# A decoder layer on one core: feed-forward units taken in pairs, seven block products in place of eight

## The chip, the core and the metric

The kernel runs on one core of a Trainium2 chip. The engines named here are PE (TensorE, matmuls into PSUM), DVE (VectorE), ACT (ScalarE), POOL (GpSimd) and SP, which only issues transfers between DRAM and SBUF. Each engine takes its instructions in a fixed order and waits, at each, until what the instruction needs is there. The metric is device microseconds of one execution, lower is better; the median of three runs before is 626.39 us (626.0 to 626.81).

## The reference

One layer of a decoder on 256 tokens of width 1024, in float32: two mixers (blockwise attention and a gated recurrence), cross-attention to 256 memory tokens, a SwiGLU feed-forward part with 2816 hidden columns, and a final norm. What the change touches is the feed-forward part:

```
hn = rmsnorm(h, norm_ffn_g[l])
gu = hn @ w_ffn_in[l]
h = h + (jax.nn.silu(gu[..., :FFN_HIDDEN]) * gu[..., FFN_HIDDEN:]) @ w_ffn_out[l]
return rmsnorm(h, final_norm_g)
```

## The kernel before, in words

**Chunks.** All weights are laid out as 97 chunks of 1 MB, a tile of 128 x 2048 each, in the order of use (`ORDER`, from `plan`). Chunks 0 to 63 belong to the stages ahead of the feed-forward part, 33 to it. A chunk is loaded by SP into a `raw` tile (two buffers), and then split into two float32r tiles: `hi`, a rounded copy by ACT (L193), and `lo`, the rest, raw minus hi (L197). Both are made in two halves; of each half of 1024 columns DVE computes 576 of `lo` and POOL 448 (in the first nine chunks DVE computes all). There are three buffers of `hi` and of `lo`. A product of two float32 matrices is then three float32r matmuls, hi by hi, lo by hi and hi by lo (`mm3t`, L236 to L239). `nxt` (L204) hands out the next chunk and first prepares all chunks up to two ahead (`LEAD`).

**The feed-forward part.** The hidden columns are cut into 11 units of 256. A unit's input chunks `("I", o, kh)` hold 512 of the 1024 rows (`kh` is the half) and its 256 gate and 256 up columns. For both halves `kh` and both halves `t` of the tokens (128 each), `ffn_in` adds 4 x 3 matmuls of 128 x 512 into the PSUM tile `psi` of that `t`: 24 matmuls for a chunk. The normed input stands transposed as `h2h` and `h2l` (made from `h2g` in `turn_h2`); its scale by token, `r`, is applied behind the product. `gate` (L1092) makes `fu` = silu(r * gate) * (r * up), by one row of ACT and one of DVE. `turn_hid` transposes the two `fu` of a unit on PE (`hidT`) and splits them into `hid`. The unit's output chunk `("O", o)` is 2 x 1024; `ffn_out` adds its 24 matmuls into four PSUM tiles `acc` that stay for the whole part. The order on PE is: the two input chunks of unit o, with the transposes of unit o - 1 between them, then the output chunk of unit o - 1.

**Order.** PE's order is that of the code. For the other engines a scheduler decides, except in the last few lines of the kernel. PSUM is eight banks: four in the pool `mm`, where `psi` and `hidT` are, and four in `sm`, where `acc` is in this part.

Of the kernel before, what the change touches and what calls it, by code (L numbers as in the profile page):

```python
# [10 lines left out]
F32 = mybir.dt.float32  # L11
# [56 lines left out]

ORDER = plan()


# [46 lines left out]
def build(tc, A, out):  # L118
    nc = tc.nc
    V, SC, G, PE, SY = nc.vector, nc.scalar, nc.gpsimd, nc.tensor, nc.sync  # L120
    with ExitStack() as ctx:
# [43 lines left out]
        ready = {}  # L165
        made, at = [0], [0]

        def prep(tags=None, raw=None):
            i = made[0]
            made[0] += 1  # L170
            first = i < 2
            if raw is None:
                raw = wr.tile([128, 2048], F32, name="raw", tag="raw")
            if tags is None:
# [11 lines left out]
            if sent == 1:  # L186
                SY.dma_start(raw, A["w"][i])
            for c in range(pieces):
                a = slice(c * n, (c + 1) * n)
                if i == 0:  # L190
                    SY.dma_start(raw[:, a], piece(A["w"][i], a))
                    yield
                SC.activation(hi[:, a], raw[:, a], AF.Copy)  # L193
                cut = (c + 1) * n - (0 if i in ALONE else POOL_COLS // pieces)
                for eng, b in ((V, slice(c * n, cut)), (G, slice(cut, (c + 1) * n))):
                    if b.start < b.stop:
                        eng.tensor_tensor(lo[:, b], raw[:, b], hi[:, b].bitcast(F32), op=ALU.subtract)  # L197
            ready[i] = (hi, lo)

        def run(g):  # L200
            for _ in g:
                pass

        def nxt(lead=LEAD):  # L204
            i = at[0]
            at[0] += 1
            while made[0] <= min(i + lead, len(ORDER) - 1):
                run(prep())
            return ready.pop(i)

# [24 lines left out]

        def mm3t(ps, xh, xl, h, l, first, last):  # L236
            PE.matmul(ps, xh, h, start=first, stop=False)  # L237
            PE.matmul(ps, xh, l, start=False, stop=False)  # L238
            PE.matmul(ps, xl, h, start=False, stop=last)  # L239

# [821 lines left out]
        def wo_part(ps, t, c, kh):  # L1062
            t_part(ps, wo[2 * c + kh], (oxh, oxl), t, kh)

        def turn_h2(t, c):
# [8 lines left out]
            G.tensor_tensor(h2l[:, ks, ts], g, h2h[:, ks, ts].bitcast(F32), op=ALU.subtract)  # L1074

        todo = None
# [10 lines left out]

        ring = ("B7", "B14", "B10", "B11", "B12", "B6")
        X2 = (h2h, h2l)
        hid, acc, two, psi, hm = {}, {}, {}, {}, {}  # L1090

        def gate(o, t):  # L1092
            r, ps = two["r"][:, t:t + 1], psi.pop((o, t))
            g = t2("fg", (128, 256))
            SC.activation(g, ps[:, 0:256], AF.Silu, scale=r)  # L1095
            u = t2b("fu", (128, 256))
            V.scalar_tensor_tensor(u, ps[:, 256:512], r, g, op0=ALU.mult, op1=ALU.mult)  # L1097
            hm[o, t] = u

        def turn_hid(o):  # L1100
            bk = mm.tile([128, 2, 256], F32, name="hidT", tag="mm")
            for t in range(2):
                u = hm.pop((o, t))
                for j in range(2):
                    PE.transpose(bk[:, j, t * 128:(t + 1) * 128], u[:, j * 128:(j + 1) * 128], ident)
            hd = big(ring[o % 6], "hid", (128, 2, 2, 256), F32R)
            split(bk, hd[:, 0], hd[:, 1])
            hid[o] = hd

        def ffn_in(o, kh, t, w):  # L1110
            if kh == 0:
                psi[o, t] = mm.tile([128, 512], F32, name="psi", tag="mm")
            t_part(psi[o, t], w, X2, t, kh)

# [9 lines left out]

        def ffn_out(o):
            w = by_k(nxt(), 2)
            for t in range(2):
                for c in range(2):
                    out_part(o, w, t, c)

        for u in ORDER[at[0]:-2]:
            if u[0] == "O":
                ffn_out(u[1])
                continue
            _, o, kh = u
            w = by_k(nxt(), 4)
            for t in range(2):
                ffn_in(o, kh, t, w)
                if (o, kh, t) == (0, 0, 0):
                    turn_h2(1, 1)  # L1140
                    two["r"] = rstd2(ssq2, "h2")
                if kh == 1:
                    gate(o, t)
            if kh == 0 and o:
                turn_hid(o - 1)

# [18 lines left out]
        ssq3 = cp.tile([128, 5], F32, name="ssq3")  # L1165
        hg3 = {i: big(ring[j], "hg3", (128, 512)) for j, i in enumerate(((0, 0), (0, 1), (1, 0)))}
        v3 = cp.tile([128, 3], F32, name="v3")
# [94 lines left out]
```

## Time and profile before

| | |
|---|---|
| median of the runs | 626.39 us |
| span of the profiled execution | 624.0 us |
| outside the span | 2.4 us |
| first feed-forward matmul | 432.0 us |
| mean granted clock of TensorE | 0.997 |
| DMA | 107.5 MB, mean 172 GB/s |

The span is one profiled execution, from its first instruction to its last. In the rows of groups, the columns are: line, engine, operation, out<-in, shapes, count, then busy us and mean ns of one, then the idle time before them and what ended it. A tile's rows give minimum, median and maximum of the duration in ns, then the first and last start. A timeline row begins with start and duration in us. Lines of the kernel before and of the changed kernel differ; L193 before is L257 after, L197 is L261, L279 is L347.

### The profile page before, as it was taken

Reading aid. Unit: us, or ns where it says so; the run is one execution under the profiler, and the core shown is the slowest. Engines: PE = TensorE matmul, PEld = TensorE weight load, DVE = VectorE, ACT = ScalarE, POOL = GpSimd, SP = SyncE. Lnnn points to the kernel's source line nnn. Section 1 sums busy time; section 2 is a strip of 40 time slices with the busy share of each in tenths; the row PEclk is TensorE's granted clock in tenths of the full one; section 3 lists DMA queues with packets and bytes.
Section 4 is the critical chain, followed back from the end, with each engine's and each line's share of the span. In section 5 each row is a group of like instructions: output and inputs, shape, how many; then the busy total and the mean of one; then the engine's idle time right before and its main releaser. Section 6 shows DMA issues by size and latency. Waiting matters only on the chain.

```text
span 624.0 us, 8466 instructions
## 1 busy us (share of the span) xinstructions
PE 615.9 (99%) x3135; PEld 512.5 (82%) x3135; DVE 384.2 (62%) x672; ACT 331.4 (53%) x533; POOL 372.4 (60%) x296
## 2 busy tenths in 40 slices
PE   9999999999999999999999999999999999999995
PEld 7888888888877877778888889888888888888884
DVE  7566678979766875748856456754444444444433
ACT  7775554234376756727457556644543444434432
POOL 3887844556544464355867876656655665566553
PEclk9999999999999999999999999999999999999998
DMA  9755443334443333545455544453344555454511
GB/s 345 296 204 202 155 182 135 135 135 140 185 149 135 136 135 134 204 169 183 156 207 189 183 175 189 140 199 134 132 178 171 195 203 187 166 190 198 203 68 67
DMA packets 16888, 107.50 MB, mean 172 GB/s; under 512 B 2000, under 2 KB 2640, under 8 KB 4560
## 3 DMA queue, kind: packets, MB, share of 16 engines
q1 hardware_dynamic: 16128, 106.14, 46.5%
q10 hardware_dynamic: 720, 0.84, 0.4%
q8 instruction: 24, 0.39, 0.3%
q14 instruction: 16, 0.13, 0.1%
HBM read 105.92 MB, written 1.05 MB: 171 GB/s over the span
## 4 chain that ended last, share of the span: by engine, by line
PE 98%; DVE 0%; POOL 0%; issue 0%; POOLq 0%; DVEq 0%
PE pst L237 14%; PE pst L239 14%; PE pst L238 14%; PE psi L237 6%; PE psi L239 6%; PE psi L238 6%; PE psf L252 5%; PE acc L237 3%; PE acc L239 3%; PE acc L238 3%; PE psf L253 2%; PE lp L616 2%; PE psg L510 1%; PE pso L237 1%; PE pso L239 1%; PE pso L238 1%
## 5 line engine op out<-in xcount | busy, mean ns | idle before, releaser
L197 POOL TENSOR_TENSOR lo<-raw,hi 128x448 fp32r<-128x448 f32 x172 | 272.6, 1602 | 182.1 <-ACT hi L193 169.6
L193 ACT ACTIVATE hi<-raw 128x1024 fp32r<-128x1024 f32 (+1 forms) x194 | 195.7, 1036 | 165.9 <-PE pst L239 58.9
L197 DVE TENSOR_TENSOR lo<-raw,hi 128x576 fp32r<-128x576 f32 (+2 forms) x194 | 198.1, 1027 | 133.6 <-ACT hi L193 131.6
L237 PE MATMUL pst<-hi,Xh 128*128 128x512 f32 x256 | 103.2, 403 | 0.0
L239 PE MATMUL pst<-hi,Xl 128*128 128x512 f32 x256 | 99.9, 390 | 0.0
L238 PE MATMUL pst<-lo,Xh 128*128 128x512 f32 x256 | 99.8, 390 | 0.0
L237 PE MATMUL psi<-hi,h2h 128*128 128x512 f32 x176 | 69.6, 395 | 0.0
L239 PE MATMUL psi<-hi,h2l 128*128 128x512 f32 x176 | 68.7, 390 | 0.0
L238 PE MATMUL psi<-lo,h2h 128*128 128x512 f32 x176 | 68.5, 389 | 0.0
L239 PEld LDWEIGHTS pst<-hi,Xl 128*128 128x128 f32 x256 | 48.0, 188 | 10.4
L237 PEld LDWEIGHTS pst<-hi,Xh 128*128 128x128 f32 x256 | 48.1, 188 | 9.9 <-issue 0.7
L238 PEld LDWEIGHTS pst<-lo,Xh 128*128 128x128 f32 x256 | 48.1, 188 | 9.3
L239 PEld LDWEIGHTS psi<-hi,h2l 128*128 128x128 f32 x176 | 33.0, 188 | 7.1
L238 PEld LDWEIGHTS psi<-lo,h2h 128*128 128x128 f32 x176 | 33.1, 188 | 6.6
L237 PEld LDWEIGHTS psi<-hi,h2h 128*128 128x128 f32 x176 | 33.1, 188 | 6.5
L237 PE MATMUL acc<-hi,hid 128*128 128x512 f32 x86 | 33.6, 390 | 0.0
L239 PE MATMUL acc<-hi,hid 128*128 128x512 f32 x86 | 33.5, 389 | 0.0
L238 PE MATMUL acc<-lo,hid 128*128 128x512 f32 x86 | 33.5, 389 | 0.0
L1097 DVE SCALAR_TENSOR_TENSOR fu<-psi,r_h,fg 128x256 f32<-128x256 f32 x22 | 10.6, 484 | 26.0 <-ACT fg L1095 26.0
L1095 ACT ACTIVATE fg<-psi,r_h 128x256 f32<-128x256 f32 x22 | 10.4, 475 | 29.9 <-PE psi L239 29.9
L252 PE MATMUL psf<-H,hi 128*128 128x512 f32 x64 | 22.8, 400 | 0.0
L252 PE MATMUL psf<-M,hi 128*128 128x512 f32 x64 | 22.5, 396 | 0.0
(344 smaller groups left out, 1120.9 us busy)
## 6 DMA issues: line engine op xcount, KB each, us to landing
raw<-w SPq DMA_DIRECT2D x94, 1024.0 KB, 4.8
raw<-w SPq DMA_DIRECT2D x4, 512.0 KB, 6.1
raw<-w SPq DMA_DIRECT2D x4, 256.0 KB, 4.1
H<-xtok SPq DMA_DIRECT2D x1, 1024.0 KB, 9.2
mraw<-mT SPq DMA_DIRECT2D x1, 1024.0 KB, 5.0
xraw<-xT SPq DMA_DIRECT2D x1, 512.0 KB, 6.1
gfin<-gfin SPq DMA_DIRECT2D x1, 512.0 KB, 3.7
out<-H SPq DMA_DIRECT2D x2, 256.0 KB, 2.0
```

The lines of the kernel that those rows point to most:

```text
L193: SC.activation(hi[:, a], raw[:, a], AF.Copy)
L197: eng.tensor_tensor(lo[:, b], raw[:, b], hi[:, b].bitcast(F32), op=ALU.subtract)
L237: PE.matmul(ps, xh, h, start=first, stop=False)
L238: PE.matmul(ps, xh, l, start=False, stop=False)
L239: PE.matmul(ps, xl, h, start=False, stop=last)
L252: PE.matmul(ps, w[0][:, k, a], X2[:, :, k], start=k == 0, stop=False)
L253: PE.matmul(ps[:, 0], w[1][:, k, a], X2[:, 0, k], start=False, stop=k == 7)
L510: PE.matmul(pss[c][t], z[:, k, t * 128:(t + 1) * 128], ws[c][0][:, k], start=z is Xh and k == 0, stop=False)
L616: PE.matmul(ps[:, j], KS[:, a0 + j], QQ[:, a0 + j, 0:n], start=True, stop=True)
L1095: SC.activation(g, ps[:, 0:256], AF.Silu, scale=r)
L1097: V.scalar_tensor_tensor(u, ps[:, 256:512], r, g, op0=ALU.mult, op1=ALU.mult)
```

## The change

**Products.** Unit 0 stays as it was. Units 1 to 10 become five pairs (a, b) (`PAIRS`). For a pair, tokens (two halves), rows (two halves) and units (two) make a product of 2 x 2 blocks by 2 x 2 blocks, which took eight block products of 12 matmuls (half an input chunk's work each). It is now done with seven, in Winograd's form of Strassen's scheme. Four of the seven left sides are sums of the blocks of `h2g`; `token_sums` makes and splits them once (`ts`, `Sh`). The right sides are four chunks as they are and three sums of chunks.

**Sums of chunks.** For each pair two sums of two chunks are made in DRAM (`summed`), by POOL's transfers: a copy of one chunk and then a transfer that adds another. These 20 transfers are issued one at each odd chunk from 9 to 47 (`block_sums`, called in `nxt`). Product 5 loads the first sum (and, beside it, the chunk of product 3) into a double tile `raws`. Product 6's weights are `raws[0]` plus `raws[1]`, added by DVE over 2048 columns (L218); product 4's are that plus one more chunk, which a transfer of POOL adds into SBUF (L221). Product 7 loads the second sum.

**Banks and gates.** Products 1, 6, 7 and 4 add up in one PSUM tile, `b1`; ACT copies it on the way, behind products 1, 6 and 7 (`fc`). Product 2 is in `b2`; products 5 and 3 add up in `b3`. DVE combines copies and banks into the four blocks of gate and up columns. The order on PE is 1, 2, 5, 6, an output chunk, 7, an output chunk, 4, 3, with the transposes of the pair before behind 1 and 2; in the first pair there is one output chunk, behind 7. `gate` now makes two rows of ACT (silu, and a scaled copy of up) and multiplies on POOL.

**Buffers.** In this part every second `raw` goes to two more buffers (`more`, at the places of two tiles that held the weights of the stage just ahead), so there are four. `hid` has four places in place of six. DVE computes all columns of `lo` from chunk 64 on, and POOL none.

```diff
+AT_CHUNK = {u: i for i, u in enumerate(ORDER)}
+PAIRS = [(o, o + 1) for o in range(1, NF // 2, 2)]
...
+        part = [("g", g, p) for p in range(1, 8)]
+        p1, p2, p3, p4, p5, p6, p7 = part
+        if g:
+            ffn += [p1, p2, p5, p6, done[0], p7, done[1], p4, p3]
+        else:
+            ffn += [p1, p2, p5, p6, p7, done[0], p4, p3]
...
+        def block_sums():
+            for g, (a, b) in enumerate(PAIRS):
+                for i in range(2):
+                    tc.keep_in_program_order(G.dma_start(summed[g][i], A["w"][AT_CHUNK["I", b, 0]]))
+                    yield 1
+                for i, u in enumerate((("I", a, 0), ("I", b, 1))):
+                    tc.keep_in_program_order(G.dma_start(
+                        summed[g][i], A["w"][AT_CHUNK[u]], accum_op=ALU.add, max_dma_last_dim=8192))
+                    yield 1
...
+        def fresh():
+            slot[0] += 1
+            if "more" in held and slot[0] % 2:
+                return held["more"][slot[0] // 2 % 2]
+            return wr.tile([128, 2048], F32, name="raw", tag="raw")
+
+        def block(g, p):
+            a, b = PAIRS[g]
+            big_raw = held["raw"]
+            if p == 5:
+                SY.dma_start(big_raw[:, 0], summed[g][0])
+                SY.dma_start(big_raw[:, 1], A["w"][AT_CHUNK["I", b, 1]])
+                return big_raw[:, 0]
+            if p == 6:
+                V.tensor_tensor(big_raw[:, 0], big_raw[:, 0], big_raw[:, 1], op=ALU.add)
+                return big_raw[:, 0]
+            if p == 4:
+                G.dma_start(big_raw[:, 0], A["w"][AT_CHUNK["I", a, 1]], accum_op=ALU.add)
+                return big_raw[:, 0]
+            if p == 3:
+                return big_raw[:, 1]
+            raw = fresh()
+            SY.dma_start(raw, summed[g][1] if p == 7 else A["w"][AT_CHUNK["I", a, p - 1]])
+            return raw
...
-                cut = (c + 1) * n - (0 if i in ALONE else POOL_COLS // pieces)
+                cut = (c + 1) * n - (0 if i in ALONE or i >= len(HEAD) else POOL_COLS // pieces)
...
+            if 8 <= i < len(HEAD) - 4 and i % 2:
+                next(sums, 0)
...
-        ring = ("B7", "B14", "B10", "B11", "B12", "B6")
+        ring = ("B7", "B14", "B10", "B6")
...
-        def gate(o, t):
-            r, ps = two["r"][:, t:t + 1], psi.pop((o, t))
-            g = t2("fg", (128, 256))
-            SC.activation(g, ps[:, 0:256], AF.Silu, scale=r)
-            u = t2b("fu", (128, 256))
-            V.scalar_tensor_tensor(u, ps[:, 256:512], r, g, op0=ALU.mult, op1=ALU.mult)
+        held["raw"] = big("P0", "raws", (128, 2, 2048))
+        held["more"] = [big(tag, "raw", (128, 2048)) for tag in ("B11", "B12")]
+        Sh = big("P1", "Sh", (128, 2, 4, 4, 128), F32R)
...
+        def product(ps, p, w, first, last):
+            xh, xl = left(p)
+            for k in range(4):
+                mm3t(ps, xh[:, k], xl[:, k], w[0][:, k], w[1][:, k], first and k == 0, last and k == 3, not first)
+
+        def gate(o, t, src):
+            r = two["r"][:, t:t + 1]
+            g = t2("fg", (128, 2, 256))
+            SC.activation(g[:, 0], src[:, 0:256], AF.Silu, scale=r)
+            SC.activation(g[:, 1], src[:, 256:512], AF.Copy, scale=r)
+            u = pt.tile([128, 256], F32, name="fu", tag="pt")
+            G.tensor_tensor(u, g[:, 0], g[:, 1], op=ALU.mult)
...
+        for g, (a, b) in enumerate(PAIRS):
+            old = (a - 2, a - 1) if g else (0,)
+            end = g == len(PAIRS) - 1
+            b1 = mm.tile([128, 512], F32, name="b1", tag="mm")
+            product(b1, 1, by_k(nxt(), 4), True, True)
+            c1 = copied(b1)
+            turn_hid(old[0])
+            b2 = mm.tile([128, 512], F32, name="b2", tag="mm")
+            product(b2, 2, by_k(nxt(), 4), True, True)
+            V.tensor_tensor(c1, b2, c1, op=ALU.add)
+            gate(a, 0, c1)
+            if g:
+                turn_hid(old[1])
+            b3 = mm.tile([128, 512], F32, name="b3", tag="mm")
+            product(b3, 5, by_k(nxt(), 4), True, True)
+            product(b1, 6, by_k(nxt(), 4), False, True)
+            c2 = copied(b1)
+            if g:
+                ffn_out(old[0])
+            product(b1, 7, by_k(nxt(), 4), False, True)
+            c3 = copied(b1)
+            V.tensor_tensor(c3, b3, c3, op=ALU.subtract)
+            gate(b, 1, c3)
+            wo8 = ffn_out(old[-1], ((0, 0), (0, 1)) if end else ((0, 0), (0, 1), (1, 0), (1, 1)))
+            product(b1, 4, by_k(nxt(1 if end else LEAD), 4), False, True)
+            gate(a, 1, b1)
+            product(b3, 3, by_k(nxt(1 if end else LEAD), 4), False, True)
+            V.tensor_tensor(c2, b3, c2, op=ALU.subtract)
+            gate(b, 0, c2)
```

The rows of an engine's order give line, operation, out<-in, the shape of the output, and how often the row repeats. First DVE at the start of the feed-forward part, before: `H` is the residual, `s` and `v` lead to the norm's scale, `h2g` is the last block of the transposed input.

```order
L197 TENSOR_TENSOR lo<-raw,hi 128x576 x2
L1072 TENSOR_TENSOR h2g<-h2T,gv 128x512
L923 TENSOR_TENSOR H<-pso,H 128x512
L931 TENSOR_TENSOR s_4063<-ssq_2827 128x2
L286 TENSOR_SCALAR v__4065<-s_4063 128x2
L1072 TENSOR_TENSOR h2g<-h2T,gv 128x512
```

And now:

```order
L991 TENSOR_TENSOR H<-pso,H 128x512
L999 TENSOR_TENSOR s_4092<-ssq_2857 128x2
L354 TENSOR_SCALAR v__4094<-s_4092 128x2
L261 TENSOR_TENSOR lo<-raw,hi 128x1024 x4
L1142 TENSOR_TENSOR h2g<-h2T,gv 128x512
L261 TENSOR_TENSOR lo<-raw,hi 128x1024
L1168 TENSOR_TENSOR ts<-h2g 128x512
...
L347 TENSOR_TENSOR Sh<-ts,Sh 128x512 x4
L261 TENSOR_TENSOR lo<-raws,hi 128x1024 x2
```

Four halves of `lo` (of the second feed-forward chunk and of product 1) now stand ahead of the last `h2g`, and the token sums and their splits behind it.

Second, ACT in the part, before, from its first unit on (`fg` is the silu of the gate columns):

```order
L193 ACTIVATE hi<-raw 128x1024 x2
L1095 ACT_TABLE_LOAD
L1095 ACTIVATE fg<-psi,r_h_4067 128x256 x2
L193 ACTIVATE hi<-raw 128x1024 x3
L278 ACTIVATE hid<-hidT 128x512
L193 ACTIVATE hi<-raw 128x1024
```

Now, between two pairs; the `b` in the first row is that of product 4, the first `hi` is product 2's, `raws` is product 5's, and behind the two `hid` product 6's:

```order
L1190 ACTIVATE fg<-b_4869,r_h_4096 128x256
L1191 ACTIVATE fg<-b_4869,r_h_4096 128x256
L257 ACTIVATE hi<-raw 128x1024 x2
L257 ACTIVATE hi<-raws 128x1024 x2
L1190 ACTIVATE fg<-fc,r_h_4096 128x256
L1191 ACTIVATE fg<-fc,r_h_4096 128x256
L1237 ACTIVATE fc<-b_5115 128x512
L346 ACTIVATE hid<-hidT 128x512 x2
L257 ACTIVATE hi<-raws 128x1024 x2
L1190 ACTIVATE fg<-fc,r_h_4096 128x256
L1191 ACTIVATE fg<-fc,r_h_4096 128x256
L257 ACTIVATE hi<-raw 128x1024 x4
```

Where the splits were almost alone on ACT, gate rows, a bank's copy and both `hid` of the old pair now stand among them.

Third, DVE in the part, before, from its first unit on:

```order
L197 TENSOR_TENSOR lo<-raw,hi 128x576 x2
L1097 SCALAR_TENSOR_TENSOR fu<-psi,r_h_4067,fg 128x256 x2
L197 TENSOR_TENSOR lo<-raw,hi 128x576 x3
L279 TENSOR_TENSOR hid<-hidT,hid 128x512
L197 TENSOR_TENSOR lo<-raw,hi 128x576
```

And now, between two pairs; the row of L1267 combines product 3's bank, that of L218 is the sum of the two raw tiles, that of L1249 combines product 2's bank:

```order
L261 TENSOR_TENSOR lo<-raw,hi 128x1024 x4
L1267 TENSOR_TENSOR fc<-b_4934,fc 128x512
L261 TENSOR_TENSOR lo<-raws,hi 128x1024 x2
L347 TENSOR_TENSOR hid<-hidT,hid 128x512
L218 TENSOR_TENSOR raws<-raws 128x2048
L1249 TENSOR_TENSOR fc<-b_5146,fc 128x512
L347 TENSOR_TENSOR hid<-hidT,hid 128x512
L261 TENSOR_TENSOR lo<-raws,hi 128x1024 x2
L261 TENSOR_TENSOR lo<-raw,hi 128x1024 x6
```

Between the splits of products 5 and 6 stand two `hid`, the raw sum and a combination.

More of the change, by code (lines that the diff above doesn't have):

```diff
@@ L166, in build @@
         made, at = [0], [0]
+        dram = pool("dram", 1, space=bass.MemoryType.DRAM)
+        summed = [[dram.tile([128, 2048], F32, name="sum%d_%d" % (g, i), tag="sum%d_%d" % (g, i))
+                   for i in range(2)] for g in range(len(PAIRS))]
+        def block_sums():
[7 more added lines that the diff above has]
+                    yield 1
+        held, slot = {}, [0]
+        def fresh():
[21 more added lines that the diff above has]
+            return raw
         def prep(tags=None, raw=None):
@@ L171, in prep @@
             first = i < 2
-            if raw is None:
-                raw = wr.tile([128, 2048], F32, name="raw", tag="raw")
+            loaded = STREAM[i][0] == "g"
+            if loaded:
+                raw = block(*STREAM[i][1:])
+            elif raw is None:
+                raw = fresh()
             if tags is None:
@@ L185, in prep @@
                 SY.dma_start(raw[:, a], piece(A["w"][i], a))
-            if sent == 1:
-                SY.dma_start(raw, A["w"][i])
+            if sent == 1 and not loaded:
+                SY.dma_start(raw, A["w"][STREAM[i][1]])
             for c in range(pieces):
@@ L202, in run @@
                 pass
+        sums = block_sums()
         def nxt(lead=LEAD):
@@ L234, in mm3, with mm3t @@
             PE.matmul(ps, ll, rh, start=False, stop=last)
[L236 to L239, printed above, removed]
+        def mm3t(ps, xh, xl, h, l, first, last, more=False):
+            PE.matmul(ps, xh, h, start=first, stop=False, skip_group_check=more)
+            PE.matmul(ps, xh, l, start=False, stop=False, skip_group_check=more)
+            PE.matmul(ps, xl, h, start=False, stop=last, skip_group_check=more)
         def by_k(w, k):
@@ L1136, in build @@
+        for kh in range(2):
             w = by_k(nxt(), 4)
             for t in range(2):
-                ffn_in(o, kh, t, w)
-                if (o, kh, t) == (0, 0, 0):
+                if kh == 0:
+                    psi[t] = mm.tile([128, 512], F32, name="psi", tag="mm")
+                t_part(psi[t], w, X2, t, kh)
+                if kh == 0 and t == 0:
                     turn_h2(1, 1)
                     two["r"] = rstd2(ssq2, "h2")
+                    token_sums()
                 if kh == 1:
-                    gate(o, t)
@@ L1144, in build, with copied @@
-            if kh == 0 and o:
-                turn_hid(o - 1)
+                    gate(0, t, psi[t])
+        def copied(ps):
+            c = t2("fc")
+            SC.activation(c, ps, AF.Copy)
+            return c
+        for g, (a, b) in enumerate(PAIRS):
+            old = (a - 2, a - 1) if g else (0,)
[26 more added lines that the diff above has]
+            gate(b, 0, c2)
+            if end:
+                out_part(old[1], wo8, 1, 0)
+                turn_hid(a)
+                out_part(old[1], wo8, 1, 1)
```

49 lines of the change are left out of this document (32 added, 17 removed).

## The prediction

> **What bounds the kernel now.** The page's busy table and the chain that ended last come first. The span is 624.0 us; the median of the runs is 626.39, so 2.4 us lie outside it, and I add these at the end.
>
> ```profile
> PE 615.9 (99%) x3135; PEld 512.5 (82%) x3135; DVE 384.2 (62%) x672; ACT 331.4 (53%) x533; POOL 372.4 (60%) x296
> PE 98%; DVE 0%; POOL 0%; issue 0%; POOLq 0%; DVEq 0%
> ```
>
> TensorE is busy 99% and is 98% of the chain: at present every wait of another engine is hidden behind matmuls. The stage that changes is the feed-forward part. Its windows (sum columns: window length, then the busy time of each engine) and its timeline on PE show at what pace:
>
> ```profile
> core 0: us, PE busy (x) PEld busy (x) DVE busy (x) ACT busy (x) POOL busy (x), PEclk, DMA share, GB/s
> 463.50:497.00 33.50, 33.50 (x153) 27.73 (x152) 15.26 (x19) 14.70 (x18) 20.04 (x13) 1.00 0.51 188
> ...
> 505.08 0.39 PE L237 MATMUL acc<-hi,hid 128*128 128x512 f32 x1
> ...
> 510.52 0.39 PE L237 MATMUL psi<-hi,h2h 128*128 128x512 f32 x1
> ...
> L278 ACT ACTIVATE hid<-hidT x9: 580/582/582, 450.0 to 584.4; 128x512 fp32r<-128x512 f32 x9
> ```
>
> A matmul row says 0.39 us, but 24 of them (one output chunk) start between 505.08 and 510.52: one each 0.227 us. The duration is a pipeline's; the pace is what counts. The nine `hid` rows lie 134.4 / 8 = 16.8 us apart, so a unit takes 16.8 us: 72 x 0.227 = 16.3 and 0.4 for the transposes. In 33.5 us (two units) DVE works 15.3 and ACT 14.7: both are half idle, and POOL has 20.0.
>
> **What the change removes.** Five pairs of units need 8 half-size products each (12 matmuls), now 7. That is 5 x 12 = 60 matmuls x 0.227 = **-13.6 us**, if PE stays full. The kernel's order confirms 60 fewer rows on PE. A pair would then need 33.5 - 2.7 = 30.8 us of PE.
>
> **What it adds to DVE and ACT.** A pair has nine splits in place of six, and in this stage DVE computes the whole `lo` (POOL's 448 columns are gone).
>
> ```profile
> L197 DVE TENSOR_TENSOR lo<-raw,hi x12: 759/1239/1632, 24.5 to 49.8; 128x1024 fp32r<-128x1024 f32 x10, 128x576 fp32r<-128x576 f32 x2
> 472.06 2.00 ACT L193 ACTIVATE hi<-raw 128x1024 fp32r<-128x1024 f32 x2
> L279 DVE TENSOR_TENSOR hid<-hidT,hid 128x512 fp32r<-128x512 f32 x9 | 6.2, 685 | 0.0
> L1095 ACT ACTIVATE fg<-psi,r_h 128x256 f32<-128x256 f32 x22 | 10.4, 475 | 29.9 <-PE psi L239 29.9
> L927 ACT ACTIVATE hjunk<-H 128x512 f32<-128x512 f32 x4 | 2.5, 628 | 7.1 <-DVE H L923 7.1
> ```
>
> From the early splits, where DVE also does all 1024 columns, half a `lo` costs 1.24, about 1.15 when one follows the other. DVE per pair: 18 x 1.15 = 20.7; the 2048-wide sum of two raw tiles as two halves, 2.2; three combinations and two `hid` rows at 0.69, 3.4; together 26.3 of 30.8 us. ACT: nine splits at 2.0, three copies at 0.6, eight gate rows at 0.45, two `hid` at 0.58: 24.6 of 30.8. Both fit on average, but neither is half idle any more, and both take their rows in a fixed order. So I walk the places where that order meets PE.
>
> **Between two pairs.** Zero is where PE ends product 4 of the old pair. PE then does product 3 (to 2.7), product 1 (5.45), the transposes (5.8), product 2 (8.5), transposes (8.9), product 5 (11.6), and product 6 is due at 11.6. ACT: two gate rows to 0.9, split of product 2's chunk to 2.9, of product 5's to 4.9. DVE follows in the order shown: `lo` 2 from 1.95 to 4.3, the product 3 combination 4.9, `lo` 5 to 7.2, `hid` 7.9, the raw sum 10.0, the product 1 combination 10.7, `hid` 11.3, and only then the first half of `lo` 6, 12.4. PE's second matmul of product 6 wants it at 11.85: **0.6 late**. What is late next is the output chunk behind it: its second half of `lo` ends at 16.3 where PE wants it at 15.9, **0.4**. So 1.0 us a pair, with DVE in an unbroken chain. Into that chain come two of POOL's new products (`fu`, 128x256, both inputs in SBUF):
>
> ```profile
> 473.14 0.76 DVE L197 TENSOR_TENSOR lo<-raw,hi 128x576 fp32r<-128x576 f32 x1 [0.46 <-ACT hi L193]
> 474.09 1.44 DVE L197 TENSOR_TENSOR lo<-raw,hi 128x576 fp32r<-128x576 f32 x1 [0.19 <-ACT hi L193]
> L979 POOL TENSOR_TENSOR kxl<-kx,kxh 128x256 fp32r<-128x256 f32 x8 | 5.8, 737 | 1.5 <-ACT kxh L978 1.5
> ```
>
> The same DVE row takes 0.76 alone and 1.44 while a POOL row is under way: DVE waits 0.7 for it. A 128x256 row of POOL is 0.74, so one `fu` costs DVE between 0 and 0.74; I take 0.55, since the chain leaves no gap to slip into. Late per pair: 1.0 + 2 x 0.55 = 2.1, bounds 1.0 and 2.5; for the four later pairs **+8.4** (4 to 10).
>
> [...]
>
> **The first pair.** Zero is PE's start of the first feed-forward chunk. The second chunk's raw tile is one of the two extra buffers, free only about 3 us before zero, landed at 1.7 (4.8 us, rows below). DVE: its `lo` to 5.1, product 1's to 7.4, and behind these four rows `h2g`, 8.0; ACT's `h2h` 8.6, POOL's `h2l` 10.0. PE wants `h2h` at 8.55: about **1.2** late. Then the token sums and their splits hold DVE to 13 and ACT to 14.2; ACT loads the table and works the four gate rows, POOL's second `fu` is done at 18.0.
>
> ```profile
> L1095 ACT ACT_TABLE_LOAD x1 | 1.3, 1283 | 0.7 <-PE psi L239 0.7
> L1180 POOL TENSOR_TENSOR hg<-H,gfin 128x512 f32<-128x512 f32 x3 | 3.9, 1289 | 8.8 <-DVE H L1172 8.7
> ```
>
> PE stands before the transposes of unit 0 at 15.1: **3** late. Product 6 comes **0.5** late as in the later pairs. Product 7 follows it at once in the same bank, and must wait until ACT has copied it, which stands behind four halves of `hi`: **2.4**. Sum **+7**; none of these waits can be shorter than what the order puts ahead of it, but starts may overlap, so 4 to 9. At the end the last unit but one waits for its `hid`: **+0.7**.
>
> **The transfers.** Twenty 1 MB transfers of POOL now run beside the chunks 9 to 47, which lie between 59 and 322 us.
>
> ```profile
> 59.00:322.00 263.00, 262.99 (x1411) 215.23 (x1411) 195.17 (x389) 143.15 (x248) 145.48 (x105) 1.00 0.44 159
> DMA to landing us min/median/max: 3.1/4.8/7.2
> H<-xtok SPq DMA_DIRECT2D x1, 1024.0 KB, 9.2
> ```
>
> The engines are busy 0.44 x 263 = 116 us there for 41.8 MB, or 2.9 us for 1024 KB. No copy within DRAM and no adding transfer is in this trace. If a copy holds the engines 2.9 and an adding one 2.9 to 5.8, they add 58 to 87 us: a share of 0.66 to 0.77, so it fits. Chunks come each 263 / 38 = 6.9 us; with two raw buffers a load has 13.8 minus the split (2.0 on ACT and two POOL rows, 4.5) = 9.3 us, where it takes 4.8. A load that shares with a transfer takes up to 2.9 more, which fits; where chunks come each 5.8 us (270 to 322 us), 0.6 is missing three or four times. POOL issues 20 times and is 55% busy. Bounds 0 and +10 (half a us for each transfer); I take **+2**, near the lower end.
>
> In the stage itself, POOL adds a chunk to the SBUF sum. It can start when `lo` 6 is done, 14.2 on the first walk's clock. ACT stands at that chunk's `hi` from 20.8 on; behind it are two copies and gate rows, product 3's and the next product 1's split, 8.9 us of work, due at 34.4. So landing by 25.5 costs nothing: 11.3 us from issue. The nearest rows: a load, 4.8, and the slowest 1 MB, 9.2. Both inside, so **0**. SP issues product 5's two loads when the splits of products 4 and 3 have freed their tiles, about 4.5 and 0.8 us before the first walk's zero; at 4.8 they land at 0.3 and 4.0, and are wanted at 2.9 (by `hi`) and 7.9 (by the raw sum): 2.6 us of room, also **0**. The other loads of SP's queue find their buffers free earlier.
>
> Sum: -13.6 + 8.4 + 7 + 0.7 + 2 = **+4.5**: span 628.5, time **631**.
>
> **The rivals.** *The adding transfer is too slow.* Past 11.3 us each us costs one per pair, five in all, as ACT cannot pass the waiting `hi`. An addition reads two operands: engines held 5.8, alone 7.7, beside loads that take half the engines up to 1.9 + 11.6 = 13.5. That is 2.2 x 5 = 11 more: 642; at 16 us, 655. Nothing in the trace excludes it. [...]
>
> *The queues keep up (faster).* The place is DVE's chain before product 6: all of the lateness after the first pair hangs on ten rows being 0.6 to 1.7 us too long for PE's 9.7. If `fu` finds gaps and the rows run at their shortest, the later pairs lose nothing, the first 4: -13.6 + 4 + 0.7 + 1 = -8: 618. It decides from a chain below 9.7 us. For it: the averages fit (26.3 and 24.6 of 30.8); against it: the order, with the raw sum ahead of `lo` 6.
>
> *The transfers hold up the stages before.* POOL's issue or the shared engines cost 0.5 to 1 us each: 639 to 649. Against it: 9.3 us of room.
>
> *The product form does not hold:* PE could need more than 0.227 where the stationary side changes source; the unit's 16.3 shows no such thing, so it has next to no chance.
>
> **How the numbers follow.** Forecast case (625 to 637): 0.45; the queues keep up: 0.26; slow adding: 0.21; transfers before: 0.07; other, the product form among it: 0.02. A measurement tells 0.2%, 1.25 us, from no change. Below 625.1 lie the faster rival and a little of the forecast: 0.28. Within 1.25 us: 0.12 of the forecast. Slower: the rest, 0.6. The range leaves out the lowest and highest tenth: below 616, near the full gain of 612.8, and above 653. The likeliest case alone spans 625 to 637.
>
> **What would show it.** PE busy falls by 60 matmuls. In the waits of the new profile PE should stand before `b` (product 6) for `lo` on DVE, about 0.5 to 1.5 us a pair, before the first `hidT` for POOL's `fu`, and before product 7 for ACT's copy. DVE should be near 85% in a pair's window. The landing time of `raws<-w` on POOL's queue decides the first rival: under 11 us it is wrong. If PE shows no wait in the later pairs, my chain is too long by its step of `fu` or the raw sum; if PE waits before 320 us, the transfers' step is wrong.

## The result, and the profile after

| | before | after |
|---|---|---|
| median of the runs | 626.42 us (626.0 to 626.81) | 635.13 us (634.06 to 636.21) |
| span of the profiled execution | 624.0 us | 634.1 us |
| first feed-forward matmul | 432.0 us | 440.4 us |
| from there to PE's last matmul | 185.2 us | 186.6 us |

The changed kernel takes 1.0139 times as long (95% interval 1.0124 to 1.0154): 8.7 us more. The forecast was 631, in a range of 616 to 653; the direction was right and the size 4 us short. The table already says where it was short: 8.4 of the 10.1 us between the two spans were lost ahead of the part that was rewritten.

The page of after, busy time and share by engine (PE has its 60 matmuls fewer):

```profile
PE 611.0 (96%) x3075; PEld 500.8 (79%) x3075; DVE 448.9 (71%) x708; ACT 377.7 (60%) x604; POOL 301.7 (48%) x277
```

PE was busy 99% before; now some waits show. The waits of PE in after, first from 20 to 430 us, then from 440 us on (engine, tile and line; whom it waited for; us in total, times, the longest):

```profile
PE mT L933 <- POOL tat L928: 3.7, 3, 2.2
PE pst L307 <- DVE ml L347: 1.2, 2, 1.0
PE pst L305 <- ACT mh L346: 0.7, 1, 0.7
...
PE hidT L1201 <- POOL fu L1193: 2.9, 2, 2.6
PE b L306 <- DVE lo L261: 2.1, 5, 0.8
PE b L305 <- ACT fc L1237: 2.0, 1, 2.0
PE psi L307 <- POOL h2l L1144: 0.9, 1, 0.9
PE acc L306 <- DVE lo L261: 0.7, 4, 0.2
PE acc L307 <- DVE hid L347: 0.2, 1, 0.2
```

The second group is the prediction's list, wait for wait: the last norm block (`h2l`), the first `hidT` behind `fu`, product 6 behind `lo` five times, product 7 behind the copy `fc`, the output chunk behind `lo` four times, the last unit but one behind its `hid`. The first group should hardly be there. Its place is 297 to 322 us, the end of the mixer: `tat` is its gated output, which POOL completes and PE transposes (`mT`). Side by side, that stretch before and after (columns: length, busy time of PE, weight loads, DVE, ACT, POOL, then clock, share of the DMA engines, GB/s), with the time of a chunk's load (`raw<-w`) from issue to landing there, and ACT's waits for loads; first before, then after:

```profile
262.00:325.00 63.00, 63.00 (x303) 51.59 (x303) 42.67 (x56) 33.89 (x51) 41.91 (x27) 1.00 0.51 190
raw<-w SPq DMA_DIRECT2D x10, 1024.0 KB, 4.8
ACT hi L193 <- DMA raw<-w: 4.9, 1, 4.9
```

```profile
262.00:325.00 63.00, 57.49 (x266) 45.22 (x266) 40.64 (x53) 29.50 (x44) 37.80 (x28) 1.00 0.71 229
raw<-w SPq DMA_DIRECT2D x9, 1024.0 KB, 7.2
sum<-w POOLq DMA_DIRECT2D x3, 1024.0 KB, 11.1
ACT hi L257 <- DMA raw<-w: 19.6, 5, 5.3
```

PE is idle 5.5 us in this window, a load lands after 7.2 us in place of 4.8, and ACT stands five times, not once, waiting for one. In after's timeline (start, duration, engine) one such late load reaches PE in this way:

```profile
293.19 2.01 ACT L257 ACTIVATE hi<-raw 128x1024 fp32r<-128x1024 f32 x2 [1.68 <-DMA raw<-w]
```

```profile
294.33 3.36 POOL L261 TENSOR_TENSOR lo<-raw,hi 128x448 fp32r<-128x448 f32 x2 [5.75 <-ACT hi L257]
297.63 0.54 POOL L195 DMA_DIRECT2D sum<-w  x1
298.19 1.28 POOL L928 TENSOR_TENSOR tat<-tat,tbt 128x512 f32<-128x512 f32 x1
```

ACT's `hi` starts when the load has landed, POOL's `lo` waits for `hi`, and `tat` stands behind `lo` in POOL's order; PE's first wait before `mT` ends with this `tat`. Counted by the same matmuls (back from the first feed-forward one), after is 0.8 us behind at 11 us, 1.1 at 293, 7.9 at 324 and 8.4 at 432. The first 0.8 is no part of the change: other runs of kernels with the same beginning have -0.1 to +1.0 there.

Last, the pairs, counted from the transposes at the head of one to those of the next. In after the third, fourth and fifth pair begin theirs at 521.31, 553.35 and 585.37, so a pair takes 32.0 us, where two units took 33.6 before. One pair's window shows DVE at 26.25 of 32.00, or 82% (the prediction said 85):

```profile
521.30:553.30 32.00, 31.53 (x141) 25.32 (x140) 26.25 (x25) 23.46 (x32) 5.21 (x5) 1.00 0.78 274
```

### The profile page after: what moved, and what is told of

It reads as the page before. It is cut to its first block, busy times and chain, and to the rows that moved or that the text cites. A ratio compares the mean times of both kernels' runs of the same rounds, so it can differ in the third digit from the quotient of the medians.

```text
span 634.1 us, 8476 instructions
## 1 busy us (share of the span) xinstructions
PE 611.0 (96%) x3075; PEld 500.8 (79%) x3075; DVE 448.9 (71%) x708; ACT 377.7 (60%) x604; POOL 301.7 (48%) x277
## 5 line engine op out<-in xcount | busy, mean ns | idle before, releaser
L261 DVE TENSOR_TENSOR lo<-raw,hi 128x576 fp32r<-128x576 f32 (+2 forms) x184 | 202.6, 1122 | 81.5 <-ACT hi L257 80.3
L257 ACT ACTIVATE hi<-raw 128x1024 fp32r<-128x1024 f32 (+1 forms) x184 | 183.7, 1035 | 110.6 <-PE pst L307 52.5
L261 POOL TENSOR_TENSOR lo<-raw,hi 128x448 fp32r<-128x448 f32 x106 | 161.5, 1537 | 110.7 <-ACT hi L257 89.1
L1193 POOL TENSOR_TENSOR fu<-fg 128x256 f32<-128x256 f32 x22 | 24.1, 1094 | 137.3 <-ACT fg L1191 90.1
L261 DVE TENSOR_TENSOR lo<-raws,hi 128x1024 fp32r<-128x1024 f32 x40 | 47.6, 1220 | 24.0 <-ACT hi L257 24.0
L257 ACT ACTIVATE hi<-raws 128x1024 fp32r<-128x1024 f32 x40 | 40.6, 1052 | 26.3 <-DMA raws<-w 21.6
L306 PE MATMUL b<-lo,Sh 128*128 128x512 f32 x80 | 32.3, 404 | 2.1 <-DVE lo L261 2.1
L305 PE MATMUL b<-hi,Sh 128*128 128x512 f32 x80 | 32.4, 405 | 2.0 <-ACT fc L1237 2.0
L307 PE MATMUL acc<-hi,hid 128*128 128x512 f32 x86 | 33.6, 391 | 0.2 <-DVE hid L347 0.2
L305 PE MATMUL acc<-hi,hid 128*128 128x512 f32 x86 | 33.7, 392 | 0.0
L307 PE MATMUL b<-hi,Sh 128*128 128x512 f32 x80 | 31.9, 399 | 0.0
L305 PE MATMUL b<-hi,h2h 128*128 128x512 f32 x60 | 23.9, 398 | 0.0
L307 PE MATMUL b<-hi,h2l 128*128 128x512 f32 x60 | 23.5, 391 | 0.0
L306 PE MATMUL b<-lo,h2h 128*128 128x512 f32 x60 | 23.4, 390 | 0.0
```

Source lines behind the costliest of these rows:

```text
L305: PE.matmul(ps, xh, h, start=first, stop=False, skip_group_check=more)
L306: PE.matmul(ps, xh, l, start=False, stop=False, skip_group_check=more)
L307: PE.matmul(ps, xl, h, start=False, stop=last, skip_group_check=more)
L1193: G.tensor_tensor(u, g[:, 0], g[:, 1], op=ALU.mult)
```

## The experiments

Three questions: why the stages before lose 7 us, what sets a later pair, and what sets the first pair. Medians are beside runs of the kernel before on the same chip (626.1 to 626.6). Periods and waits are from the one execution of each kernel that was profiled; single waits of PE are counted from start to start of its matmuls, less 0.227, and so are 0.1 to 0.2 longer than the profile's list gives them.

### The stages before: traffic, or POOL's work of issuing it

**Small transfers.** The same 20 issues, a sixteenth of the rows each.

```diff
-G.dma_start(summed[g][i], A["w"][AT_CHUNK["I", b, 0]])
+G.dma_start(summed[g][i][0:8], A["w"][AT_CHUNK["I", b, 0]][0:8])
...
-SY.dma_start(big_raw[:, 0], summed[g][0])
+SY.dma_start(big_raw[:, 0], A["w"][AT_CHUNK["I", b, 0]])
```

> The 20 transfers of POOL stay where they are, but each moves 8 of 128 rows (a sixteenth), and products 5 and 7 load a plain chunk in place of the sums, so the result of the five pairs is left out of what is right. POOL's issues stay, the traffic goes. Theory A (POOL's issuing, 0.5 to 0.8 us each, and its place ahead of the rows of tat): the stages before stay late, first feed-forward matmul at 438 to 441, time 633 to 636. Theory B (the traffic makes the loads of raw late, 7.2 us to landing in 262 to 325 where a load took 4.8, and from there ACT's hi, POOL's lo and tat): first feed-forward matmul at 432 to 433.5, loads of raw in that window below 5.5, no wait of PE before mT, time 627 to 629.

Measured: 629.54 us, ratio 1.0049 (1.0033 to 1.0065). The first feed-forward matmul is at 434.3, which is 2.3 later than before: 1.0 comes from the beginning, 0.4 is lost between 293 and 324 us in place of 6.8, and 0.9 elsewhere (0.7 in after). So this matmul and the time lie above theory B's ranges, by 0.8 and 0.5. That window in this run, and its loads:

```profile
262.00:325.00 63.00, 62.84 (x301) 50.96 (x300) 42.74 (x58) 32.97 (x52) 43.32 (x31) 1.00 0.54 190
raw<-w SPq DMA_DIRECT2D x11, 1024.0 KB, 4.8
sum<-w POOLq DMA_DIRECT2D x5, 64.0 KB, 5.1
```

POOL issues as often as in after, each issue takes it 0.5 to 0.9 us as there, and PE is busy again. So in this window it is the traffic (theory B): the loads are back at 4.8 us. POOL's issuing is worth 0.4 us at most here.

**Other places for the transfers.** Three kernels differ from after in one line, the condition on the chunk number `i`:

```diff
-if 8 <= i < len(HEAD) - 4 and i % 2:
+if i % 2 and (8 <= i < 38 or i > 48) and i < len(HEAD) - 4:   # first kernel
+if 8 <= i < 38 and i % 3:                                      # second
+if 6 < i < 36 and i % 3:                                       # third
```

> The whole computation; the transfers skip the odd chunks 39 to 47, and the last five go to chunks 49 to 57. Theory B (traffic where the gated mixer's end, mraw and gfin load too and chunks come each 5.8 us): the 6.6 us between 297 and 322 go, time 628 to 630. If each transfer costs a share wherever it lies, the five cost about as much in cross-attention, time 633 to 635. If POOL's own rows are what counts, cross-attention has POOL rows (kxl, qxl) that PE needs, and the waits appear before these.

> The whole computation; all 20 transfers lie at chunks 8 to 37 (two of three chunks, before: the odd ones from 9 to 47), where the first 15 cost 0.3 us in the run before, and none where chunks come each 5.8 us. Theory B (a transfer costs nothing where chunks come each 6.9 us, since a load then has 9.3 us; it costs where they come faster): first feed-forward matmul at 433 to 434, the wait before mT gone, time 627.5 to 629.5. Rival (the engines are filled at two transfers in three chunks, a share of 0.8, and loads queue up there): waits of PE for lo before 270 us, 3 to 8 us, time 631 to 636.

> The whole computation; the 20 transfers lie at chunks 7 to 35 (two of three). With them at 8 to 37, the load before chunk 43 still landed about 2 us late, and a wait before mT of 1.5 us was left. Theory (only the last transfer, at chunk 37, reached into the fast stretch): the wait before mT goes, first feed-forward matmul at 433.5 to 435, time 629.5 to 631. Rival (that wait is the scheduler's, and not the traffic's): 1.5 to 1.9 us are lost between 293 and 324 again, time 631.5 to 633.

| transfers at chunks | median | ratio to before | first feed-forward matmul | lost between 293 and 324 us | lost elsewhere in these stages |
|---|---|---|---|---|---|
| 9 to 47, odd (after) | 635.13 | 1.0139 | 440.4 | 6.8 | 0.7 |
| 9 to 37 and 49 to 57, odd | 636.43 | 1.0153 (1.0128 to 1.0178) | 440.1 | 1.7 | 6.1, of it 4.2 at 376 us |
| 8 to 37, two of three | 632.17 | 1.0086 (1.0070 to 1.0101) | 436.2 | 1.9 | 1.7 |
| 7 to 35, two of three | 634.19 (630.5 to 637.2) | 1.0121 (1.0076 to 1.0166) | 434.8 | 0.0 | 2.8 |

The first row shows that the price follows the traffic: five transfers moved into cross-attention cost there about what they had cost in the mixer, before a new wait for POOL's `qxl` (1.6 of the 4.2 us there are PE at half its clock behind that wait; see the last section). Neither of the last two places is free, though the second kernel is 3.0 us faster than after. Its theory is missed; its time is in the rival's range, but PE's wait ahead of 270 us is 0.7 and not 3 to 8. Closer together, the transfers hold up a load between 150 and 175 us (in the third kernel ACT waits 8.6 us for one), and PE waits for the mixer's `ra`, 0.7 us in the second kernel and 1.5 in the third:

```profile
PE rT L819 <- POOL ra L814: 1.5, 1, 1.5
```

The third kernel's profiled execution did what its theory said (no wait before `mT`, 630.5 us), but it was the fastest of four, and the others took 633.7 to 637.2. What they lost was not profiled. The price does vary: eight other runs of this study keep the transfers where after has them, and lose 4.6 to 9.2 us between 293 and 324. In three of them (6.7, 8.3 and 9.2) PE also runs at half its clock there, behind the waits, for 3.4 or 6.8 us; that is 1.6 to 1.9 us of the loss.

### A later pair

**No raw sum.** DVE's addition of two raw tiles for product 6 is left out.

```diff
-V.tensor_tensor(big_raw[:, 0], big_raw[:, 0], big_raw[:, 1], op=ALU.add)
+pass
```

> The sum of two raw tiles for product 6 is left out (its weights are then product 5's once more, and the result is not the layer's). DVE has 2.28 us less in each pair. Theory (DVE's chain): no wait in the later pairs, pair at 30.8 to 30.9 us. If ACT's chain behind PE's end of product 4 sets the pair, product 6 still waits, and the pair stays over 31.3.

Measured: no wait of PE between 505 and 600 us, and this window of one pair, transposes to transposes:

```profile
513.80:544.70 30.90, 30.90 (x141) 25.56 (x140) 24.58 (x24) 23.53 (x32) 5.23 (x5) 1.00 0.81 273
```

The pair takes 30.9 us, the prediction's 30.8 for full PE. So the seven products cost PE what was worked out, and all that a later pair loses, 1.15 us, goes with the raw sum. The run does not say by which way. Without the sum DVE has 2.28 us less to do, and ACT can make product 6's `hi` sooner; in after the two are ready together (DVE is through with `hid` at 527.11, the first half of `hi` at 527.05). The one execution took 624.9 us, though it lost 6.0 in the stages before. In the first pair, too, a wait got shorter, that of product 7, which is 2.0 in after:

```profile
PE b L305 <- ACT fc L1237: 0.7, 1, 0.7
```

**Half of the raw sum on POOL.**

```diff
-V.tensor_tensor(big_raw[:, 0], big_raw[:, 0], big_raw[:, 1], op=ALU.add)
+[e.tensor_tensor(big_raw[:, 0, h], big_raw[:, 0, h], big_raw[:, 1, h], op=ALU.add)
+ for e, h in ((V, slice(0, 1024)), (G, slice(1024, 2048)))]
```

> The whole computation; of the raw sum for product 6, DVE adds the first 1024 columns and POOL the second 1024 at the same time. Theory (the later pairs are set by DVE's unbroken chain, which gets 1.1 us shorter): product 6's wait of 0.45 and the output chunk's 0.35 both go, pair 30.8 to 31.2 in place of 32.05, -3 to -5 in all, time 630 to 632. Rival (ACT sets them: from PE's end of product 4 two gate rows, hi 2, hi 5 and hi 6 in a row): only product 6's wait gets shorter, -1 to -2, time 633 to 634. Rival 2 (POOL's addition is too slow, over 3 us beside DVE): product 6's second half waits, 0 to +2.

Measured: 646.16 us, ratio 1.0311 (1.0287 to 1.0336); the pairs behind the first take 36.7, 35.2 and 33.7 us (in after 32.5, 32.0 and 32.0). This is the second rival, and worse than it said. The first two of these pairs hold a stretch of 3.4 us each at a granted clock of 0.50, the third has none. POOL and DVE around the sum, by the timeline (start, duration, engine):

```profile
528.20 3.43 POOL L218 TENSOR_TENSOR raws<-raws 128x1024 f32<-128x1024 f32 x1
```

```profile
528.15 1.21 DVE L218 TENSOR_TENSOR raws<-raws 128x1024 f32<-128x1024 f32 x1
529.28 0.68 DVE L1249 TENSOR_TENSOR fc<-b,fc 128x512 f32<-128x512 f32 x1
532.75 2.36 DVE L261 TENSOR_TENSOR lo<-raws,hi 128x1024 fp32r<-128x1024 f32 x2 [2.78 <-ACT hi L257]
```

POOL's row is given as 3.43 us; its shortest in this run is 2.375. It begins 0.05 after DVE's and is 1.06 longer than that shortest one, near DVE's 1.21; it ends 2.27 after DVE's row, as if it had begun when that one was through. Then ACT, and DVE behind it, stand until POOL has ended.

**Gate rows later.** ACT's gate rows of product 4 are written behind product 3 in four pairs.

```diff
-gate(a, 1, b1)
 product(b3, 3, by_k(nxt(1 if end else LEAD), 4), False, True)
+gate(a, 1, b1)
```

> The whole computation; in four pairs the gate rows of product 4 are written behind product 3, so that ACT makes hi of product 2 ahead of them, and DVE starts its chain about 1 us sooner. Theory (DVE's unbroken chain from lo 2 to the output chunk sets the later pairs): product 6's wait of 0.45 and the output chunk's 0.35 go, -0.8 a pair, -3 to -4 in all, pair 30.8 to 31.2, time 631 to 632. Rival (the waits hang on the way from the raw sum over hi to lo of product 6): the same, since both start sooner. If the pair's period of 32.05 is set by something else than these two waits (the clock, the transposes), time stays at 634 to 636.

Measured: 635.89 us, ratio 1.0150 (1.0126 to 1.0174), pair 31.9; the second pair took 37.3 in place of 32.5, of it 6.8 us at a granted clock of 0.50. In the pairs behind it the two waits went, and another came, of the same size:

```profile
PE b L305 <- DVE hid L347: 2.2, 3, 0.8
```

Product 5's bank `b3` now waits 0.8 us in each of three pairs until DVE has made `hid`, that is, until the bank of transposes is read that it takes over: in the new order DVE has the raw sum ahead of that `hid`. The sum is also longer here, 2.72 in place of 2.28 us. It stands right behind `lo`, and POOL's `fu`, which had started under `lo`, runs until 524.12:

```profile
523.55 2.72 DVE L218 TENSOR_TENSOR raws<-raws 128x2048 f32<-128x2048 f32 x1
```

So by these rows about half of the new wait is the 0.44 us by which the sum is longer beside `fu`; the other half is the wait that moved with the rows. No run takes them apart.

**`fu` on DVE.**

```diff
-G.tensor_tensor(u, g[:, 0], g[:, 1], op=ALU.mult)
+V.tensor_tensor(u, g[:, 0], g[:, 1], op=ALU.mult)
```

> The whole computation; the gate's product fu goes from POOL to DVE. The prediction's term (each of two fu a pair holds DVE 0.55, and POOL's row is 0.74 long while DVE waits): DVE's own row of about 0.35 costs less than that, so the later pairs get shorter or stay, 31.5 to 32.1 us. What the rows of after say (POOL's fu waits 0.4 to 1.1 for DVE, DVE's rows keep their length, so fu costs DVE nothing): DVE's chain gets 0.35 longer for each fu that stands in it, pair 32.3 to 33.2 us, time +1 to +4 on 635 but for the first pair, whose transposes get fu sooner.

Measured: 634.19 us, ratio 1.0124 (1.0100 to 1.0148), pair 32.2. Product 6 waits 0.78 in place of 0.45, the output chunk 0.26 in place of 0.35: 0.2 us a pair more. That is between the two expectations, nearer the second. For these pairs the direction speaks against the prediction's term, and the timeline of after shows why. POOL, then DVE:

```profile
521.93 1.79 POOL L1193 TENSOR_TENSOR fu<-fg 128x256 f32<-128x256 f32 x1 [4.15 <-PE hidT L1201]
```

```profile
520.76 2.35 DVE L261 TENSOR_TENSOR lo<-raws,hi 128x1024 fp32r<-128x1024 f32 x2
523.03 0.68 DVE L347 TENSOR_TENSOR hid<-hidT,hid 128x512 fp32r<-128x512 f32 x1
523.63 2.28 DVE L218 TENSOR_TENSOR raws<-raws 128x2048 f32<-128x2048 f32 x1
```

`fu` is given as 1.79 where a free one is 0.73: it begins under a running `lo`, and ends 0.6 after that. DVE's rows keep their lengths here: what follows `lo` is `hid`, and it takes 0.68 beside `fu` (DVE's eleven `hid` in after take 0.675 to 0.692). It is not so everywhere. Ahead of the second pair two rows of `lo` begin under a `fu` that is already running, and take 1.77 and 1.66 in place of 1.22 us. POOL, then DVE, for the first of them:

```profile
481.54 1.65 POOL L1193 TENSOR_TENSOR fu<-fg 128x256 f32<-128x256 f32 x1 [13.01 <-ACT fg L1191]
```

```profile
482.51 1.77 DVE L261 TENSOR_TENSOR lo<-raw,hi 128x1024 fp32r<-128x1024 f32 x1
```

Of `fu` and `lo`, the one that starts second is the longer one in all these rows.

**A plain load for product 4.**

```diff
-G.dma_start(big_raw[:, 0], A["w"][AT_CHUNK["I", a, 1]], accum_op=ALU.add)
+G.dma_start(big_raw[:, 0], A["w"][AT_CHUNK["I", a, 1]])
```

> POOL's transfer into SBUF for product 4 loads the chunk without adding, so the result is not the layer's. Theory (the adding one has room: 8.7 us to landing, 11.3 allowed): landing 5 to 7, the later pairs stay at 32.0. If the adding transfer held the pairs (ACT stands idle 3.8 us at hi of product 4 until it lands), they get 0.5 or more shorter.

Measured, in one execution of 635.5 us: landing 5.1 us in place of 8.7, the later pairs at 32.0 as in after. The adding transfer costs these pairs nothing. (The lateness in the stages before is 10.1, so the times can't be compared.)

```profile
raws<-w POOLq DMA_DIRECT2D x5, 1024.0 KB, 5.1
```

The first two pairs are another matter. From the first feed-forward matmul to the third pair's transposes it is 79.0 us here, 80.9 in after, and 80.6 to 81.5 in the six other kernels that keep the token sums, the raw sum, the adding transfer and the gate rows' place. ACT's wait for product 4's chunk between 440 and 500 us, in after and here:

```profile
ACT hi L257 <- DMA raws<-w: 5.6, 1, 5.6
```

```profile
ACT hi L257 <- DMA raws<-w: 2.2, 1, 2.2
```

Behind that wait ACT and DVE are late in after until product 6 of the second pair, which waits 0.95 there and 0.50 here. So about 2 us of the first two pairs hang on the adding transfer, as far as one execution can say.

### The first pair

**Another order.** Unit 0's transposes go behind product 2, its output chunk between products 6 and 7.

```diff
-ffn += [p1, p2, p5, p6, p7, done[0], p4, p3]
+ffn += [p1, p2, p5, p6, done[0], p7, p4, p3]
...
-turn_hid(old[0])          # behind product 1
+turn_hid(old[0])          # behind product 2
```

> The whole computation; only the first pair's order on PE is changed: the transposes of unit 0 behind product 2 (before: product 1), and its output chunk between products 6 and 7 (before: behind 7). The walk's theory (hidT waits for POOL's fu 2.8 + 0.3, product 7 for ACT's copy 2.1, both only because of the order): both waits go, -5 us, time 629.5 to 631. Rival (DVE and ACT are a chain in the first pair, and what one place gains the next loses): the output chunk or product 7 waits for lo, -1 to -2.5, time 632.5 to 634.

Measured: 634.77 us, ratio 1.0129 (1.0114 to 1.0144). PE's waits from 440 to 484 us:

```profile
PE b L305 <- ACT fc L1237: 2.7, 1, 2.7
PE b L305 <- ACT hi L257: 2.1, 1, 2.1
PE psi L307 <- POOL h2l L1144: 0.9, 1, 0.9
PE b L306 <- DVE lo L261: 0.8, 1, 0.8
PE hidT L1201 <- POOL fu L1193: 0.3, 1, 0.3
```

`hidT` waits 0.3 now, but product 6 waits for `hi` (2.1) and the copy's wait went from product 7 to product 4 (2.7). In all nothing is gained: the rival, though the time came 0.8 above its range.

**No token sums.**

```diff
-token_sums()
+pass
```

> The sums of token blocks and their splits are left out; the four products take plain blocks of the normed input as left sides, so the result is not the layer's. Theory (the first pair's waits, 7 us in all, are DVE's and ACT's lateness from these rows, 5.5 on DVE): hidT's 3.1 goes to under 0.5 and product 7's 2.1 gets shorter, first pair 4 to 6 us shorter. Rival (the waits hang on the order alone: fu asked for too soon, the copy behind four hi): hidT's wait stays above 2, product 7's stays.

Measured, in one execution of 633.9 us, PE's waits from 442 to 485 us:

```profile
PE b L305 <- ACT fc L1237: 2.0, 1, 2.0
PE psi L307 <- POOL h2l L1144: 0.8, 1, 0.8
PE b L306 <- DVE lo L261: 0.6, 1, 0.6
```

The 3.1 before `hidT` is gone, so it came from the sums' rows on DVE and ACT; product 7's wait for the copy stays at 2.0, so it is not theirs. Each theory holds for one of the two waits. But the rival's "order alone" goes too far for product 7: without the raw sum its wait was 0.7. From the first feed-forward matmul to PE's last one it is 183.6 us, 3.0 less than after. The first pair is 4.7 shorter, since the stretch at half clock is gone with `hidT`'s wait, and the second is 1.7 longer: the second of the two transposes in it now waits 1.3 for `fu`.

**Order, halves and POOL together.** The half sum on POOL, `hidT` behind product 2, unit 0's output chunk in two halves around product 7, the combination of product 2 behind product 6.

```diff
+[e.tensor_tensor(...) for e, h in ((V, slice(0, 1024)), (G, slice(1024, 2048)))]
...
+wo8 = ffn_out(old[0], ((0, 0), (0, 1)))              # ahead of product 7
+V.tensor_tensor(c1, b2, c1, op=ALU.add)
...
+ffn_out(old[-1], ((1, 0), (1, 1)), wo8)              # behind product 7
```

> The whole computation; the one before with the first pair's order changed as well: unit 0's transposes behind product 2, half of its output chunk between products 6 and 7 and half between 7 and 4, and the combination of product 2 written behind product 6. Against the run with the half sum on POOL: theory (the first pair's waits come from copies and fu that are asked for too soon, and each has now 2.7 us more): hidT's 3.1, product 7's 2.1 and the slower clock behind it (1.4) go, -4 to -6, time 625 to 628. Rival (ACT and DVE are filled in the first pair by the token sums and four splits, so the time is only found elsewhere, as when the order was changed alone): -1 to -2, time 629 to 631.

Measured: 645.78 us, ratio 1.0308 (1.0272 to 1.0344). Against the kernel with the half sum alone nothing is gained: from the first feed-forward matmul to the transposes at the head of the second pair it is 53.3 us, there 49.4, and the second pair is shorter by 3.2. PE's longest wait in the first pair, ACT's, and POOL's transfer in the timeline:

```profile
PE b L305 <- ACT fc L1237: 5.6, 1, 5.6
```

```profile
ACT hi L257 <- DMA raws<-w: 7.9, 1, 7.9
```

```profile
464.80 0.95 POOL L221 DMA_DIRECT2D raws<-w  x1 [2.72 <-DVE lo L261]
```

ACT stands 7.9 us at `hi` of product 4, until 475.5, when POOL's adding transfer has landed, 10.6 us after its start, and the copy that PE needs is queued behind it. This is the mechanism of the prediction's first rival, in a place where the transfer starts late and its reader stands ahead of a copy.

## Why the prediction came out as it did

| term | predicted | measured in after |
|---|---|---|
| 60 matmuls fewer | -13.6 | 33.6 - 30.9 = 2.7 a pair: -13.5 |
| four pairs behind the first | +8.4 (2.1 each) | 32.05 - 30.9 = 1.15 each, and 0.5 more in the second: +5.1 |
| first pair | +7 | waits 1.0 + 3.1 + 0.6 + 2.1 = +6.9 |
| the slower clock behind a wait | - | +1.6 |
| end | +0.7 | +0.3 before the last matmul, +0.3 behind it |
| SBUF's adding transfer | 0 | no row of its own; about 2 of the rows above hang on it |
| SP's loads of product 5 | 0 | 0 |
| stages before | +2 (0 to 10) | +7.6 |
| beginning, no part of the change | - | +0.8 |

The measured rows add up to 9.1 of the 10.1 us between the spans; the other 1.0 has no place of its own (the matmuls next to a wait often come 0.1 us late). The predicted ones make +4.5.

**Right: the matmuls.** The products cost PE 0.227 us a matmul with either source of weights; without the raw sum a pair is at 30.9 with PE full.

**Right: where PE stands in the feed-forward part.** The waits were named, each with its releaser, and the first pair's 6.9 us are near the walk's 7. What makes them is only in part the order: `hidT`'s wait is the token sums' work. Product 7's outlives the token sums, but falls from 2.0 to 0.7 when the raw sum goes: then ACT makes product 6's `hi` without waiting, and what is left is little more than the copy itself, 0.6.

**Wrong for the later pairs: the step of `fu`.** "I take 0.55, since the chain leaves no gap to slip into" cost 1.1 us of the 2.1 for a later pair. Without it the walk's 1.0 (0.6 for product 6, 0.4 for the output chunk) meets 1.15. The price was read off two DVE rows, one of 0.76 "alone" and one of 1.44 beside POOL. But the first was not alone: a POOL row began 0.05 behind it and took 1.73, and the second had itself started behind that POOL row. So in these rows, `hid` with its 0.68 left aside, who pays is a matter of who starts second. In the chain of a later pair it is POOL: `fu` 1.79 in place of 0.73; in the half sum, too, it is POOL's row, 3.43 in place of 2.38. Where it is DVE, the runs show a price near the prediction's: 0.55 and 0.44 on the two `lo` ahead of the second pair, 0.44 on the raw sum when the gate rows come later. That the price falls on DVE in each pair was the prediction's assumption, and the runs do not bear it out.

**Right for the later pairs, not for the first: the adding transfer into SBUF.** It takes 8.7 us, under the 11.3 allowed, and a plain load, at 5.1, changes nothing in the later pairs. The first rival's 5.8 us of the engines for an addition was an estimate that no run shows; the landings were 8.7 against 5.1 us. The room was the better argument. It was worked out on a later pair's clock alone. In the first pair ACT comes to the chunk 5.6 us before it has landed, and about 2 us of the first two pairs' waits hang on it.

**Wrong in size: the transfers in the stages before**, +2 where 7.6 came (inside the term's own bounds of 0 and +10), and this is where the forecast's 4 us are missing. The step that was mis-sized is "A load that shares with a transfer takes up to 2.9 more, which fits; where chunks come each 5.8 us (270 to 322 us), 0.6 is missing three or four times." The loads did grow by about that (4.8 to 7.2 in the middle), but room was counted per load. What followed was not 0.6 each: a late load delays ACT's `hi`, then POOL's `lo`, then, in POOL's fixed order, `tat`, for which PE stands. The prediction had this as a rival of 0.07 and ruled that it had "9.3 us of room"; the window of 262 to 325 us needed its own walk, as the feed-forward part got one. Its test, "if PE waits before 320 us, the transfers' step is wrong", is what the profile shows.

That the time came within 4 us of the forecast is in part luck, because the two largest wrong sizes pulled apart: 3.3 us too much for the pairs behind the first, 5.6 too little in the stages before; the slower clock, 1.6, was in no term. The range is 37 us wide and would have held either alone. (The chances of the five cases add up to 1.01, not 1.) "The queues keep up", the faster rival, needed a shorter chain ahead of product 6: with the raw sum taken out it comes true for the later pairs, and the one execution of that kernel was at 624.9. No kernel here that computes the layer beats the one before.

## What to carry to other kernels

The transfers added in the background were paid for where the loads beside them were already tight (there a load took 7.2 us in place of 4.8, and 6.8 us were lost), so walk the tightest stretch that such a transfer crosses, row by row behind a late load, as carefully as the stage that was rewritten. Before charging one engine for a row of another beside it, look which of the two starts second in the new order, and whether the row got longer in such a place (`lo`, 1.77 in place of 1.22) or did not (`hid`, 0.68). A transfer's room must be worked out where its reader comes earliest, here in the first pair (5.6 us before the landing). In DVE's unbroken chain taking the raw sum out paid (1.15 us a pair), and the one move of rows within it that was tried moved the wait (0.8 us).

## What was not expected of the hardware

Behind some of its waits PE ran at half its clock, for 3.4 or 6.8 us. In after, product 7 waits 2.1 us, 3 us behind a wait of 0.6; soon after, eight matmuls come 0.427 us apart, not 0.227, 1.6 us in all, and the granted clock says the same, 0.50 from 471.3 to 474.6. In the kernel with transfers in cross-attention such a stretch follows a wait of 2.1 us with one of 0.2 ahead. First the window in after, then in that kernel:

```profile
470.70:474.50 3.80, 3.78 (x10) 3.02 (x11) 1.44 (x2) 0.00 (x0) 0.00 (x0) 0.58 0.98 213
```

```profile
381.00:383.50 2.50, 2.50 (x9) 2.11 (x9) 2.50 (x3) 0.00 (x0) 1.57 (x2) 0.50 1.10 305
```

Each of these two costs 1.6 us, and those of the three runs that have one between 293 and 324 us 1.6 to 1.9. Not each such wait is followed by one: behind 2.8 + 0.3 before `hidT` in after the granted clock is 1.00 from 458 to 468. Before, whose one wait of PE in the list is 1.6 us at the very start (`warm`), is granted 1.00 until PE's last matmul. No run shows how long a wait must be for it; product 7's 2.1 us in after cost PE 3.7 with what came behind.
